# A decoder layer on one core: where the last query head's means, the sample constants and the low key halves are placed, and how sums of sample pairs are split up

## The chip, the cores and the metric

The kernel runs on one core of a Trainium2 chip. Its time is the device time of one execution in microseconds, as the median of the runs. All arithmetic is in the kernel; the host only lays arrays out.

## The reference

One layer of a hybrid decoder with shared weights for two groups of requests: a prompt of 1024 tokens (batch 1) and 8 sampling requests of 8 tokens each with 4096 cached positions. Everything is float32, the model width is 1024. Cut to what matters:

```python
h = rms_norm(x, norm1) * (1 + scale1) + shift1          # scale, shift: from a conditioning vector
z = h @ w_in
q, kc, vc, ks, vs, kw, vw, gates, conv_bg, conv_cg, conv_h, pool_in = split(z)
q  = rms_norm(q per head of 64, q_gain); ks, kw likewise
k_cmp, v_cmp = compress(all raw keys / values, blocks of 32, stride 16)
o_cmp, p_cmp = cmp_attention(q, k_cmp, v_cmp)
top_i, ok    = select_blocks(p_cmp)                      # 16 blocks of 64 keys
o_slc = slc_attention(q, top_i, ok, ks, vs)
o_win = window_attention(q, kw, vw)                      # 512 positions
o = g0 * o_cmp + g1 * o_slc + g2 * o_win
x = x + gate1 * (concat[o, short_conv, multi_pool] @ w_out)
x = x + gate2 * swiglu(rms_norm(x, norm2) * (1 + scale2) + shift2)
```

There are 8 query heads and 2 key heads. A prompt token sees at most 16 blocks, so selection keeps them all there; a sample token selects 16 of 65.

## The kernel before

The kernel is written against a framework that tracks tiles, places semaphores, allocates buffers and finally orders each engine's instructions by a simulated timeline, in which an instruction traced earlier goes first among those ready. Two things bend that order: a block under `high_priority` counts as traced 2000 instructions earlier, and `issue_after(ins)` puts what a block traces on the engine of `ins` behind `ins` on that engine.

The order of tracing comes from a small planner in the kernel. Every part is a generator. It yields the time at which it can go on, by a model of the engines' times (`use` adds a cost to an engine); `run` resumes the part of lowest priority number that is ready by TensorE's model time, and moves that time on where none is. `hold(test)` yields until a test is true, in steps of 0.25 us.

Matrix products in full precision use three products of halves: `split` makes a high half by a copy to the type fp32r on ScalarE (L175) and a low half by a subtraction (`combine`, L171), on VectorE unless told otherwise.

The stages are:

1. The front: norm and modulation of h, in three chunks of tokens (384, 384 and 320 columns).
2. The input projection. For each of 16 weight tiles of 128 output channels and each chunk, `project` accumulates 8 x 3 products in one bank. The last four tiles are q0 to q3, each of two query heads. Each chunk of a query or key tile then goes through `head_norm`: squares (ScalarE, L757), means by a product with a constant matrix `mean_h` (TensorE), root (ScalarE, L762), reciprocal (VectorE, L765), and scaling (VectorE, L766), which reads the projection's bank again. `heads` counts these, `last_scale` is the last scaling. Meanwhile compression (`compress`) of cached pages goes on, three of eight batches in this stage.
3. Attention. `attention` makes the masks (GpSimd and VectorE), `key_stacks` splits the two sets of prompt keys (j = 0 selection, j = 1 window; 1024 columns and 64 compressed ones each) into `kh` and `kl`, `query_parts` splits the queries of a tile of 128 tokens into `qh` and `ql`. `constants3` makes masks and index matrices for the sample tokens (`rsum`, `m_new`, `m_win`, `sel`, `hind`), `sample_setup` lays out their queries and new keys (`qb`, `kn`). Then three parts share the engines:
   - the prompt: 32 units (8 query tiles, 2 halves of the heads, selection or window branch). `scores` runs the products into banks of the tag S (six of them), evacuates them with mask and minimum (VectorE, L1123), then exponential (ScalarE, L1135), reciprocal and gate (VectorE), and scales the probabilities (GpSimd, L1145). `values` transposes them and multiplies by the values.
   - the compression of the other five batches, whose products read `stream`.
   - the samples, in four pairs of requests: `sample_select` scores the compressed keys and selects blocks; 9 units per pair score pages of `cacheB` (tiles `unit` and `stream`); `sample_combine` weights the pair's eleven partial sums into `co` (L1437) and stores them. The units of a pair begin when `combined` shows that the pair before is done.
4. The output projection and the feed-forward part.

Tiles named `P` (probabilities) are allocated in a pool that opens where the projected keys lay. The planner's choice among the three parts of attention follows changing priorities, for example `1.8 + v_done / 32` for the prompt and `2 + 1.1 * u_done / 36` for the samples.

Of the kernel before, what the change touches and what calls it, by code (L numbers as in the profile page):

```python
# [17 lines left out]
P = 128  # L18
# [26 lines left out]
PACE = 0.5  # L45
EPS = 1e-6
# [16 lines left out]
class Kernel:  # L63
# [218 lines left out]
    def constants3(self, c):  # L282
        nc = self.nc
        with self.pool("ctmp") as tp:

            ti = tp.tile([P, 1], I32, name="ti")
            nc.gpsimd.iota(ti, pattern=[[0, 1]], base=0, channel_multiplier=1)
            t7 = tp.tile([P, 1], I32, name="t7")
            nc.vector.tensor_scalar(t7, ti, 7, None, op0=OP.bitwise_and)
            tv = tp.tile([P, 1], F32, name="tv")  # L290
            nc.vector.tensor_copy(tv, t7)


            di = tp.tile([P, P], I32, name="di")
            nc.gpsimd.iota(di, pattern=[[1, P]], base=P, channel_multiplier=-1)
            d7 = tp.tile([P, P], I32, name="d7")
            nc.vector.tensor_scalar(d7, di, 7, None, op0=OP.bitwise_and)
            eq = tp.tile([P, P], F32, name="eq")
            nc.vector.tensor_scalar(eq, d7, 0.0, None, op0=OP.is_equal)
            self.rsum = c.tile([P, P], F32, name="rsum")  # L300
            nc.gpsimd.memset(self.rsum, 0.0)
            for q in range(4):
                s = slice(32 * q, 32 * q + 32)
                nc.vector.tensor_copy(self.rsum[s, s], eq[s, s])


            a = tp.tile([P, 4, 64], F32, name="a")
            for b2 in range(2):
                nc.gpsimd.iota(a[64 * b2:64 * b2 + 64], pattern=[[-16, 4], [1, 64]], base=-8 * b2,
                               channel_multiplier=0, allow_small_or_imprecise_dtypes=True)  # L310
            ge = tp.tile([P, 4, 64], F32, name="ge")
            nc.vector.tensor_scalar(ge, a, 0.0, None, op0=OP.is_ge)
            ok = tp.tile([P, 4, 64], F32, name="ok")
            nc.vector.scalar_tensor_tensor(ok, a, tv[:, 0:1], ge, op0=OP.is_le, op1=OP.mult)
            self.m_new = c.tile([P, 4, 64], F32, name="m_new")
            nc.vector.tensor_scalar(self.m_new, ok, -1.0, 1e30, op0=OP.add, op1=OP.mult)


            w = tp.tile([P, 8], F32, name="w")
            nc.gpsimd.iota(w, pattern=[[1, 8]], base=0, channel_multiplier=0, allow_small_or_imprecise_dtypes=True)  # L320
            self.m_win = c.tile([P, 512], BF16, name="m_win")
            nc.gpsimd.memset(self.m_win, 0.0)
            nc.vector.tensor_scalar(self.m_win[:, 0:8], w, tv[:, 0:1], NEG, op0=OP.is_le, op1=OP.mult)


            self.sel = c.tile([P, 4, P], F32, name="sel")
            si = tp.tile([P, 4, 2, 8, 8], F32, name="si")
            for p in range(4):
                nc.gpsimd.iota(si[:, p], pattern=[[-8, 2], [0, 8], [-1, 8]], base=-64 - 16 * p,
                               channel_multiplier=1, allow_small_or_imprecise_dtypes=True)  # L330
            nc.vector.tensor_scalar(self.sel.rearrange("a p r -> a (p r)"), si.rearrange("a p b g t -> a (p b g t)"),
                                    0.0, None, op0=OP.is_equal)


            hi = tp.tile([P, 8], F32, name="hi")
            for b2 in range(2):
                nc.gpsimd.iota(hi[64 * b2:64 * b2 + 64], pattern=[[-8, 8]], base=0, channel_multiplier=1,
# [2037 lines left out]
```

## Time and profile before

| | |
|---|---|
| median of 3 runs | 1656.8 us (1656.56 to 1657.72) |
| the profiled execution | 1654.03 us, span 1652.4 us |
| granted TensorE clock, mean over the span | 0.981 |
| busy: PE, PEld | 1565.2, 1388.2 us |
| busy: DVE, ACT, POOL | 1092.2, 775.7, 656.3 us |
| end of the input projection | 366.9 us |
| first prompt scores | 378.5 us |
| last sample products of attention | 815.8 us |

A profile shows one execution. Engines are PE (TensorE's products), PEld (its weight loads), DVE (VectorE), ACT (ScalarE), POOL (GpSimd) and SP, which issues transfers. A row of the timeline gives start, duration, engine, line, operation, the tile written and the tiles read, shapes and a count, and in brackets how long the engine had been idle before it and what ended that. L139 is the line of all plain products, L143 that of transposes, L171 and L175 those of all subtractions and copies of `split`.

### The profile page before, as it was taken

How to read it: one execution, taken by the hardware profiler on the slowest of the kernel's cores; microseconds unless marked ns; L12 is line 12 of the kernel's file. 1: busy time of each engine (PE TensorE's matmuls, PEld its weight loads, DVE VectorE, ACT ScalarE, POOL GpSimd, SP SyncE). 2: the span in 40 equal slices, each digit the busy share in tenths (PEclk: the TensorE clock that was granted, in tenths of full speed). 3: DMA queues.
4: the chain of work that ended last, by engine and by line, in shares of the span. 5: the costliest groups of instructions: out<-in, count | busy, mean ns of one | idle time of the engine just before them, and what ended most of it. 6: DMA issues, size and time to landing. Idle time of an engine off the chain costs nothing.

```text
span 1652.4 us, 35479 instructions
## 1 busy us (share of the span) xinstructions
PE 1565.2 (95%) x12569; PEld 1388.2 (84%) x12569; DVE 1092.2 (66%) x2645; ACT 775.7 (47%) x1828; POOL 656.3 (40%) x789
## 2 busy tenths in 40 slices
PE   6999999997999899899999989999999999899998
PEld 2899997895777666566699989999999999899998
DVE  4713224876555666767589878777777775577668
ACT  3522215434765667656576534343434333344444
POOL 3111110213333133222213356554544554788765
PEclk9999999998999899999999999999999999999999
DMA  9576665425467373244696565336443335967643
GB/s 339 188 266 188 193 182 169 147 77 163 136 179 219 108 211 97 78 132 126 194 319 213 189 224 185 139 137 232 147 146 138 138 136 199 380 244 249 217 159 125
DMA packets 194659, 302.12 MB, mean 183 GB/s; under 512 B 25841, under 2 KB 131634, under 8 KB 194162
## 3 DMA queue, kind: packets, MB, share of 16 engines
q1 hardware_dynamic: 175346, 272.17, 49.5%
q0 software_dynamic: 6208, 17.38, 3.3%
q10 hardware_dynamic: 12928, 10.29, 2.1%
q8 instruction: 100, 1.64, 0.4%
q14 instruction: 77, 0.63, 0.1%
HBM read 233.43 MB, written 70.53 MB: 184 GB/s over the span
## 4 chain that ended last, share of the span: by engine, by line
PE 74%; DVE 11%; ACT 5%; DMA 4%; issue 3%; POOL 2%; SPq 0%; ACTq 0%; DVEq 0%; POOLq 0%
PE bank L139 70%; PE bank L143 4%; DVE P L1123 2%; ACT P L1135 2%; DVE w_lo L171 1%; DMA w_raw<-in_wup 1%; DMA w_raw<-in_wout 1%; ACT w_hi L175 1%; DMA x<-x_d 1%; POOL P L1145 1%; POOL b_t L171 1%; DMA x<-in_xT 1%; DVE h_lo L474 1%; DVE b_lo L171 0%; DVE ml L171 0%
## 5 line engine op out<-in xcount | busy, mean ns | idle before, releaser
L139 PE MATMUL bank<-b_hi,w_hi 128*128 128x272 f32 x1232 | 351.3, 290 | 7.0 <-DVE pair L1722 2.9
L139 PE MATMUL bank<-b_lo,w_hi 128*128 128x272 f32 x1232 | 353.5, 289 | 1.7 <-DVE b_lo L171 1.7
L139 PE MATMUL bank<-b_hi,w_lo 128*128 128x272 f32 x1232 | 348.8, 288 | 1.3 <-DVE w_lo L171 0.9
L139 PEld LDWEIGHTS bank<-b_hi,w_hi 128*128 128x128 f32 x1232 | 230.5, 189 | 10.4 <-ACT b_hi L175 4.0
L139 PEld LDWEIGHTS bank<-b_lo,w_hi 128*128 128x128 f32 x1232 | 232.4, 189 | 2.4 <-DVE b_lo L171 2.3
L139 PEld LDWEIGHTS bank<-b_hi,w_lo 128*128 128x128 f32 x1232 | 230.6, 189 | 1.8 <-DVE w_lo L171 1.1
L1145 POOL TENSOR_SCALAR P<-P,st 128x128 f32<-128x128 f32 (+10 forms) x192 | 109.1, 582 | 232.7 <-DVE st L1141 141.3
L171 DVE TENSOR_TENSOR w_lo<-w_raw,w_hi 128x512 fp32r<-128x512 f32 (+2 forms) x120 | 114.6, 965 | 81.8 <-ACT w_hi L175 81.6
L171 POOL TENSOR_TENSOR w_s<-w_raw 128x512 f32<-128x512 f32 (+1 forms) x88 | 124.3, 1412 | 70.3 <-DVE w_lo L171 53.4
L175 ACT ACTIVATE w_hi<-w_raw 128x512 fp32r<-128x512 f32 (+2 forms) x122 | 80.6, 677 | 132.5 <-PE bank L139 87.7
L139 PEld LDWEIGHTS bank<-stream 128*128 128x128 f32 x1056 | 128.8, 200 | 16.0 <-issue 11.9
L139 PE MATMUL bank<-stream 128*128 128x128 f32 x1056 | 135.1, 286 | 1.8 <-DMA stream<-in_cacheA 1.1
L1135 ACT ACTIVATE P<-P,st 128x128 f32<-128x128 f32 (+12 forms) x192 | 112.7, 588 | 45.8 <-DVE st L1129 28.6
L171 POOL TENSOR_TENSOR x<-x,d_m 128x272 f32<-128x272 f32 x136 | 118.0, 887 | 34.2 <-DVE x L1925 17.5
L139 PE MATMUL bank<-h_hi,w_hi 128*128 128x384 f32 (+1 forms) x384 | 129.4, 337 | 0.4 <-DVE q L766 0.4
L139 PE MATMUL bank<-h_hi,w_lo 128*128 128x384 f32 (+1 forms) x384 | 126.6, 330 | 0.0
L139 PE MATMUL bank<-h_lo,w_hi 128*128 128x384 f32 (+1 forms) x384 | 126.4, 329 | 0.0
L171 DVE TENSOR_TENSOR w_lo<-w_s,w_hi 128x512 fp32r<-128x512 f32 (+1 forms) x124 | 115.7, 935 | 15.9 <-ACT w_hi L175 13.7
L139 PE MATMUL bank<-g,w_hi 128*128 128x272 f32 x616 | 121.4, 293 | 4.7 <-DVE x L1925 4.7
L139 PE MATMUL bank<-g,d_hi 128*128 128x272 f32 x616 | 119.1, 289 | 2.3 <-DVE x L1928 1.6
L1925 DVE SCALAR_TENSOR_TENSOR x<-bank,mod,x 128x272 f32<-128x272 f32 (+1 forms) x200 | 90.2, 476 | 39.1 <-PE bank L139 28.2
L175 ACT ACTIVATE w_hi<-w_s 128x512 fp32r<-128x512 f32 (+1 forms) x124 | 76.6, 621 | 64.5 <-PE bank L139 35.4
(376 smaller groups left out, 3756.3 us busy)
## 6 DMA issues: line engine op xcount, KB each, us to landing
g<-g_d SPq DMA_DIRECT2D x63, 544.0 KB, 6.1
g_d<-f_s SPq DMA_DIRECT2D x57, 544.0 KB, 3.4
wada<-in_wada SPq DMA_DIRECT2D x96, 256.0 KB, 5.3
stream<-in_cacheA SPq DMA_DIRECT2D x192, 128.0 KB, 3.2
w_raw<-in_wup SPq DMA_DIRECT2D x40, 512.0 KB, 4.3
unit<-in_cacheB SPq DMA_DIRECT2D x152, 128.0 KB, 2.4
stream<-in_cacheB SPq DMA_DIRECT2D x104, 128.0 KB, 2.2
w_raw<-in_wout SPq DMA_DIRECT2D x24, 512.0 KB, 5.7
```

Source lines behind the costliest of these rows:

```text
L139: return self.nc.tensor.matmul(out, lhsT, rhs, start=start, stop=stop, skip_group_check=chain)
L143: return self.nc.tensor.transpose(out, in_, self.ident if ident is None else ident)
L171: (self.nc.vector if eng == "dve" else self.nc.gpsimd).tensor_tensor(out, a, b, op=op)
L175: self.last_hi = self.nc.scalar.activation(hi, src, AF.Copy)
L474: nc.vector.scalar_tensor_tensor(lk, t, sh[:, k, 0:1], hk.bitcast(F32), op0=OP.add, op1=OP.subtract)
L1123: nc.vector.tensor_tensor_reduce(out=Pt[:, 2 * g + hl, col:col + n], in0=S[g][:, p0:p0 + n], in1=mk, scale=-1.0, scalar=3e38, op0=OP.add, ...
L1135: nc.scalar.activation(Ps, Ps, AF.Exp, scale=-1.0, bias=sy[:, g, 0:1], accum_out=sy[:, g, 1:2])
L1145: nc.gpsimd.tensor_scalar(Ps, Ps, sy[:, g, 3:4], 0.0, op0=OP.mult, op1=OP.add)
L1925: self.last_gate = nc.vector.scalar_tensor_tensor(out[:, :n], acc[:, :n], self.mod[:, 5, m, 0:1], out[:, :n], op0=OP.mult, op1=OP.add)
```

## The change

Six edits:

- `PINNED = ("q3",)`: for the last query tile, `project` is called for half of the accumulation steps; then the part holds until one more head norm has been traced, and the second half is put behind that norm's mean product (`last_mean`) on TensorE.
- `query_parts` for query tile 0 is traced ahead of `key_stacks`.
- In `key_stacks`, the low halves of the window keys (j = 1) are made on GpSimd.
- `constants3` is traced behind the second score group of the first unit, its VectorE instructions behind that group's last evacuation (`first_evac`); its scratch tiles lie in the pool of attention instead of one of their own. The sample part starts when they are traced.
- A pair's selection waits until the pair before has been selected (`selected`).
- For the first three pairs, `sample_combine` yields ahead of every third of the eleven sums.

```diff
+PINNED = ("q3",)
...
     def constants3(self, c):
         nc = self.nc
-        with self.pool("ctmp") as tp:
+        tp = c
...
-    def project(self, w, h, ch, n):
-        acc = self.bank()
-        for k in range(KT):
+    def project(self, w, h, ch, n, acc=None, ks=range(KT)):
+        acc = self.bank() if acc is None else acc
+        for k in ks:
...
-            self.mm(m[:, :n], self.mean_h, sq[:, :n], True, True)
+            self.last_mean = self.mm(m[:, :n], self.mean_h, sq[:, :n], True, True)
...
-                        acc = self.project(w, h, ch, n)
+                        if nm in PINNED:
+                            heads = self.heads
+                            acc = self.project(w, h, ch, n, None, range(KT // 2))
+                            yield from self.hold(lambda: self.heads > heads)
+                            with self.tc.issue_after(self.last_mean.ins):
+                                self.project(w, h, ch, n, acc, range(KT // 2, KT))
+                        else:
+                            acc = self.project(w, h, ch, n)
...
-                self.split(kh[:, a:a + n], kl[:, a:a + n], src, n)
+                self.stacks_at = self.split(kh[:, a:a + n], kl[:, a:a + n], src, n, eng="pool" if j else "dve")
                 yield max(self.t["dve"], self.t["act"]) - 1.0
-        self.stacks_at = max(self.t["dve"], self.t["act"])
...
+            if u == 0 and hl == 1:
+                self.first_evac = self.last_evac
+                self.scored = True
...
-        yield from self.hold(lambda: self.cmp_done >= 2 * p + 2)
+        yield from self.hold(lambda: self.cmp_done >= 2 * p + 2 and self.selected == p)
...
-        for c in range(11) if p < 3 else (8, 10, 0, 1, 2, 3, 4, 5, 6, 7, 9):
+        self.use("dve", 1.3, self.t["pe"])
+        for x, c in enumerate(range(11) if p < 3 else (8, 10, 0, 1, 2, 3, 4, 5, 6, 7, 9)):
+            if p < 3:
+                if x % 3 == 0:
+                    yield self.t["dve"]
+                self.use("dve", 0.35, self.t["pe"])
             nc.vector.scalar_tensor_tensor(o, part[:, c], w[:, c:c + 1], o, op0=OP.mult, op1=OP.add)
-        r = self.use("dve", 4.0, self.t["pe"]) + 0.5
         if p < 3:
-            yield r
+            yield self.t["dve"] + 0.3
...
     def attention(self, ap, kp_, opened):
         self.masks(ap)
         self.use("dve", 1.0)
+        self.query_parts(ap, 0)
         yield from self.key_stacks()
-        self.query_parts(ap, 0)
         with self.tc.issue_after(self.last_scale.ins):
-            self.constants3(ap)
             self.sample_setup(ap)
-        self.use("dve", 5.0)
         kp_.__exit__(None, None, None)
         pp = opened.enter_context(self.pool("prompt"))
         self.spawn(lambda: 1.8 + self.v_done / 32, self.prompt_attention(pp))
+        yield from self.hold(lambda: self.scored)
+        with self.tc.issue_after(self.first_evac.ins):
+            self.constants3(ap)
+        self.use("dve", 3.2)
+        self.constants_done = True
...
         sp = opened.enter_context(self.pool("samp", "left"))
+        yield from self.hold(lambda: self.constants_done)
         yield self.t["dve"]
```

More of the change, by code (lines that the diff above doesn't have):

```diff
@@ L283, in constants3 @@
         nc = self.nc
-        with self.pool("ctmp") as tp:
[L286 to L337, printed above, removed]
-                               allow_small_or_imprecise_dtypes=True)
-            hg = tp.tile([P, 8], F32, name="hg")
-            nc.vector.tensor_scalar(hg, hi, 0.0, None, op0=OP.is_ge)
-            self.hind = c.tile([P, 8], F32, name="hind")
-            nc.vector.scalar_tensor_tensor(self.hind, hi, 7.0, hg, op0=OP.is_le, op1=OP.mult)
@@ new lines, in constants3 @@
+        tp = c
+        ti = tp.tile([P, 1], I32, name="ti")
+        nc.gpsimd.iota(ti, pattern=[[0, 1]], base=0, channel_multiplier=1)
+        t7 = tp.tile([P, 1], I32, name="t7")
+        nc.vector.tensor_scalar(t7, ti, 7, None, op0=OP.bitwise_and)
+        tv = tp.tile([P, 1], F32, name="tv")
+        nc.vector.tensor_copy(tv, t7)
+        di = tp.tile([P, P], I32, name="di")
+        nc.gpsimd.iota(di, pattern=[[1, P]], base=P, channel_multiplier=-1)
+        d7 = tp.tile([P, P], I32, name="d7")
@@ new lines, in constants3 @@
+        nc.vector.tensor_scalar(d7, di, 7, None, op0=OP.bitwise_and)
+        eq = tp.tile([P, P], F32, name="eq")
+        nc.vector.tensor_scalar(eq, d7, 0.0, None, op0=OP.is_equal)
+        self.rsum = c.tile([P, P], F32, name="rsum")
+        nc.gpsimd.memset(self.rsum, 0.0)
+        for q in range(4):
+            s = slice(32 * q, 32 * q + 32)
+            nc.vector.tensor_copy(self.rsum[s, s], eq[s, s])
+        a = tp.tile([P, 4, 64], F32, name="a")
+        for b2 in range(2):
+            nc.gpsimd.iota(a[64 * b2:64 * b2 + 64], pattern=[[-16, 4], [1, 64]], base=-8 * b2,
+                           channel_multiplier=0, allow_small_or_imprecise_dtypes=True)
@@ new lines, in constants3 @@
+        ge = tp.tile([P, 4, 64], F32, name="ge")
+        nc.vector.tensor_scalar(ge, a, 0.0, None, op0=OP.is_ge)
+        ok = tp.tile([P, 4, 64], F32, name="ok")
+        nc.vector.scalar_tensor_tensor(ok, a, tv[:, 0:1], ge, op0=OP.is_le, op1=OP.mult)
+        self.m_new = c.tile([P, 4, 64], F32, name="m_new")
+        nc.vector.tensor_scalar(self.m_new, ok, -1.0, 1e30, op0=OP.add, op1=OP.mult)
+        w = tp.tile([P, 8], F32, name="w")
+        nc.gpsimd.iota(w, pattern=[[1, 8]], base=0, channel_multiplier=0, allow_small_or_imprecise_dtypes=True)
@@ new lines, in constants3 @@
+        self.m_win = c.tile([P, 512], BF16, name="m_win")
+        nc.gpsimd.memset(self.m_win, 0.0)
+        nc.vector.tensor_scalar(self.m_win[:, 0:8], w, tv[:, 0:1], NEG, op0=OP.is_le, op1=OP.mult)
+        self.sel = c.tile([P, 4, P], F32, name="sel")
+        si = tp.tile([P, 4, 2, 8, 8], F32, name="si")
+        for p in range(4):
+            nc.gpsimd.iota(si[:, p], pattern=[[-8, 2], [0, 8], [-1, 8]], base=-64 - 16 * p,
+                           channel_multiplier=1, allow_small_or_imprecise_dtypes=True)
@@ new lines, in constants3 @@
+        nc.vector.tensor_scalar(self.sel.rearrange("a p r -> a (p r)"), si.rearrange("a p b g t -> a (p b g t)"),
+                                0.0, None, op0=OP.is_equal)
+        hi = tp.tile([P, 8], F32, name="hi")
+        for b2 in range(2):
+            nc.gpsimd.iota(hi[64 * b2:64 * b2 + 64], pattern=[[-8, 8]], base=0, channel_multiplier=1,
+                           allow_small_or_imprecise_dtypes=True)
+        hg = tp.tile([P, 8], F32, name="hg")
+        nc.vector.tensor_scalar(hg, hi, 0.0, None, op0=OP.is_ge)
@@ L346, in ada_setup @@
+        self.hind = c.tile([P, 8], F32, name="hind")
+        nc.vector.scalar_tensor_tensor(self.hind, hi, 7.0, hg, op0=OP.is_le, op1=OP.mult)
     def ada_setup(self, pool):
@@ L2186, in build @@
         self.combined = 0
+        self.scored = self.constants_done = False
         self.n2_done = 0
@@ L2221, in build @@
         self.post_free = True
+        self.selected = 0
         self.constants2()
```

3 lines of the change are left out of this document (2 added, 1 removed).

## The prediction

> **What bounds the kernel now.** I read the page first, then the busy times of each engine by stretches of 50 us, then finer stretches where TensorE fell behind, then the waits and the timeline of that place, engine by engine.
>
> ```profile
> PE 1565.2 (95%) x12569; PEld 1388.2 (84%) x12569; DVE 1092.2 (66%) x2645; ACT 775.7 (47%) x1828; POOL 656.3 (40%) x789
> ```
>
> TensorE is busy 1565.2 us, 95% of a span of 1652.4, so time can come only from its idle 87 us and from stretches in which its clock is low. Every part of the change but the spread sums acts at the passage from the input projection to attention, so I cut that passage where its engine changes: waiting, first scores, and the work behind them. Columns are busy time (and instructions) of PE, PEld, DVE, ACT and POOL, then the granted clock, the DMA share and GB/s.
>
> ```profile
> 372.00:378.50 6.50, 0.00 (x0) 0.03 (x1) 6.50 (x9) 0.00 (x0) 3.65 (x14) 0.86 0.68 203
> 378.50:383.20 4.70, 1.98 (x15) 1.67 (x15) 4.54 (x31) 0.19 (x1) 0.00 (x0) 0.50 0.77 227
> 383.20:393.10 9.90, 9.90 (x77) 9.66 (x77) 4.02 (x34) 5.41 (x25) 5.01 (x14) 0.81 0.48 145
> ```
>
> For 6.5 us TensorE does nothing while VectorE never stops; in the next 4.7 us it works 1.98 us at half clock. That is the only stage of the kernel where VectorE sets the pace outright. The waits between 350 and 395 us name what ended TensorE's two pauses (total, times, longest), and the timeline shows where they lie:
>
> ```profile
> PE bank L139 <- DVE q L766: 6.6, 1, 6.6
> ...
> PE bank L139 <- DVE st L1123: 2.7, 1, 2.7
> ```
>
> ```profile
> 366.86 1.50 PE L139 MATMUL bank<-h_sq,mean_h 128*128 128x384 f32 x4
> 368.19 3.73 PE L139 MATMUL bank<-stream 128*128 128x128 f32 x32
> 378.50 0.89 PE L139 MATMUL bank<-kh,qh 64*128 64x192 f32 x2 [6.58 <-DVE q L766]
> ...
> 383.18 0.44 PE L139 MATMUL bank<-kh,qh 64*128 64x128 f32 x1 [2.71 <-DVE st L1123]
> ...
> 384.61 8.53 PE L139 MATMUL bank<-stream 128*128 128x128 f32 x64
> ```
>
> So 9.3 us are idle: first the scores wait for the normalised query of L766 (through the accumulator bank it reads: the operands for query tile 0 were ready before), then for the first softmax evacuation of L1123, which frees a bank. The four mean matmul pieces at 366.86 are those of q3's second and third chunk, both behind the whole projection. ScalarE and VectorE show why L766 is late:
>
> ```profile
> 363.83 0.48 ACT L757 ACTIVATE h_sq<-bank 128x384 f32<-128x384 f32 x1
> 367.06 0.44 ACT L757 ACTIVATE h_sq<-bank 128x320 f32<-128x320 f32 x1 [2.74 <-PE bank L139]
> 367.39 1.05 ACT L175 ACTIVATE kh<-kv__98 128x1024 fp32r<-128x1024 f32 x1
> ...
> 370.62 0.98 ACT L762 ACTIVATE h_sq<-bank,eps 128x384 f32<-128x384 f32 x2
> ```
>
> ```profile
> 368.47 1.23 DVE L171 TENSOR_TENSOR kl<-kv__98,kh 128x1024 fp32r<-128x1024 f32 x1 [1.30 <-ACT kh L175]
> ...
> 370.86 1.16 DVE L171 TENSOR_TENSOR kl<-kv__98,kh 128x1024 fp32r<-128x1024 f32 x1
> ...
> 373.37 4.55 DVE L765 RECIPROCAL h_sq<-h_sq 128x384 f32<-128x384 f32 x2
> 377.85 0.97 DVE L766 SCALAR_TENSOR_TENSOR q<-bank,qgain_s,h_sq 128x384 f32<-128x384 f32 x2
> 378.74 0.14 DVE L289 TENSOR_SCALAR t<-ti 128x1 int32<-128x1 int32 x1
> ...
> 379.67 0.48 DVE L1223 MEMSET qb<- 128x512 f32 x1
> 380.08 0.15 DVE L1230 COPY kn<-kv__98 128x128 f32<-128x128 f32 x1
> ...
> 380.55 0.57 DVE L1226 COPY qb<-q 64x256 f32<-64x256 f32 x2
> ...
> 382.65 0.28 DVE L1123 CUSTOM_DVE_ANT_0 P<-bank,m_slc 128x128 f32<-128x128 f32 x1
> ```
>
> The second chunk is squared by 364.31, yet its mean runs at 366.86 and its root at 370.62, behind all key splits on ScalarE's queue. VectorE then works without a pause from 368.47 to the first evacuation at 382.65: low key parts, two reciprocals, two scalings, the sample constants.
>
> **The change part by part.** All terms are against the profiled execution, 1654.0 us with a span of 1652.4 and 1.6 around it; the median of the runs, 1656.8, is 2.8 us more, and I put the difference on that median.
>
> *Pinned means.* The third chunk of q3 takes the 3.2 us between the squares' starts at 363.83 and 367.06. With the second chunk's mean in its middle, that mean runs near 365.0, after its square's end at 364.31, so TensorE doesn't stop; the matmuls are the same in number and cost nothing more. The root (half of 0.98, 0.5) then ends by 366.3, ahead of the splits, and one reciprocal with its scaling, (4.55 + 0.97) / 2 = 2.8, goes into the time in which VectorE waited before 368.47. By 369.2 they are done; the first low key part would have started at 368.47, so 0.7 of the 2.8 comes back. Worth 2.1 on VectorE's chain. The third chunk's mean can't be pinned to anything and stays late: its root still stands behind the splits, and it is what is late next. If the second half waited for a square delayed on ScalarE, TensorE would stop by that delay, at most the 1.05 of one split; none stands there, so I take 0 (bounds: 1.05 lost, nothing won beyond the 2.8).
>
> *Queries of tile 0 ahead of the key stacks.* The same two instructions, earlier on ScalarE and VectorE, move the key split by about half of 1.05. It is inside the 0.7; 0.
>
> *Low halves of the window keys on GpSimd.* VectorE loses the 1.16 at 370.86 and the small 64-column piece. Nearest row for the price on GpSimd, the same subtraction 1120 wide, by form:
>
> ```profile
> L171 POOL TENSOR_TENSOR wt_lo<-stream,wt_hi 128x1120 fp32r<-128x1120 f32 x2 | 5.1, 2572 | 18.5 <-ACT wt_hi L175 18.5
> ```
>
> That is 2.35 us for 1024 columns. Its first reader is the window unit behind the two first score groups, and the prompt's probability tiles lie where those keys lay, so VectorE's first evacuation now waits for GpSimd as well. GpSimd's masks fill it from the end of the projection to about 372, so the low keys are there by 374.5, before the evacuation that I expect below: gain 1.2. The price against it is that the two engines get in each other's way:
>
> ```profile
> 370.81 1.24 POOL L279 TENSOR_SCALAR_AFFINE_SELECT rowok<-rowok 128x1 f32<-128x1 f32 x1
> ```
>
> One element per lane takes 1.24 us, from 370.81 to 372.05, exactly while VectorE's subtraction of two tiles ran (370.86 to 372.02). Turned round, a 2.35 us subtraction on GpSimd can hold VectorE's own two-input work. VectorE has such work for only part of that stretch (the reciprocal has one input), so I take 1.0, with 0 and 2.35 as ends. [...]
>
> *Sample constants behind the first softmax pass.* From 378.74 to 382.65 are 3.9 us; the copies of sample queries and keys that stay take 0.48 + 0.15 + 0.57 = 1.2. So 2.7 us leave the path to the first evacuation. They come back behind it, ahead of some reciprocals of the first softmax; the 8.53 us of compression matmuls at 384.61 cover that. Were that cover gone, they would cost their 2.7. Their GpSimd instructions are ordered behind nothing and only fill that engine. The sample stream waits for the constants, so its page loads on SP's queue are issued a few us later. The timeline of that queue, and the instructions on the tile they fill (least, median and longest ns, first and last start):
>
> ```profile
> 375.51 9.82 SPq L530 DMA_DIRECT2D unit<-in_cacheB  x16
> ```
>
> ```profile
> L139 PE MATMUL bank<-unit,qb x84: 589/593/1112, 408.2 to 809.8; 128*64 128x512 f32 x84
> ```
>
> Issued from 375.51, first read at 408.2: a delay below some 20 us costs 0.
>
> *Sums in threes, and selections one after another.* The same instructions, in four groups with other work between. By form:
>
> ```profile
> L1437 DVE SCALAR_TENSOR_TENSOR co<-part,cw,co 128x128 f32<-128x128 f32 x44 | 18.8, 426 | 1.1
> ```
>
> One pair's eleven are 4.7 us of VectorE at a time when the prompt's evacuations also want it. Around the second pair's sums TensorE waited once, 2.56 us:
>
> ```profile
> 685.58 1.21 PE L143 MATMUL bank<-ident,P 64*128 64x64 f32 x32 [2.56 <-POOL P L1145]
> ```
>
> Three pairs are spread, so up to 7.7 us could be won if each had such a stall and lost it, and as much lost if the spread sums made one each. Most of the sums already had evacuations between them, so I take 0. The selections' order follows from buffers anyway: 0.
>
> *Sum.* VectorE's chain to the first evacuation shortens by 2.1 + 1.2 - 1.0 + 2.7 = 5.0 us, to about 377.7. TensorE's idle 9.3 us is bounded by that chain, so 5.0 of it goes and 4.3 stays. The clock: 1.98 us of work in the second stretch ran at 0.50 and 9.9 in the third at 0.81, so 1.0 + 1.9 = 2.9 us were lost to it. With pauses of 2 to 3 us instead of 6.6 and 2.7, I take half, 1.4 (0 and 2.9 as ends). [...] Total 6.4: 1654.0 - 6.4 = 1647.6 for a profiled execution, 1650.4 on the median. From 385 us on, all orders are laid out anew by the planner; I let the shift pass through, since TensorE remains the engine with the most work.
>
> **The rivals.** *Hardly any gain.* The third chunk's late mean, root and reciprocal set the first scores as before, and GpSimd blocks VectorE for the whole 2.35; constants are paid behind the evacuation (2.7). Left: 2.1 + 1.2 - 2.35 + 2.7 - 2.7 = 1.0, no clock gain: 1655.8. For it: the first wait is for L766, one of which still comes last. Against: one reciprocal instead of two stands there.
>
> *More gain.* Both pauses close down to what the compression matmuls can fill: 9.3 + 2.9 = 12.2 us, 1644.6. For it: 3.73 and 8.53 us of such matmuls stand ready. Against: they are bound to page loads.
>
> *Slower.* The sums in threes, spread over more softmax passes, meet GpSimd's scaling of probabilities and hold it, and TensorE waits for that, as at 685.58. Each costs 2.56; with three pairs in four groups there are twelve places. To end 3.3 us above the old time it takes 6.4 + 3.3 = 9.7 us, four such stalls; five would give 1656.8 - 6.4 + 12.8 = 1663.2. For it: their mean of 426 ns holds some much longer ones. Against: the sums met the scaling before, too.
>
> **How the numbers follow.** Likeliest, 0.57: 1650.4, own range 1647 to 1653.5 (the port price and the clock from end to end). More gain 0.11, hardly any 0.19, slower 0.13. What a measurement here can tell from no change is about 0.2%, 3.3 us: faster 0.68, same 0.19, slower 0.13. The range goes from 1644, the largest gain, to 1661, short of most of the slower case.
>
> **What would show it.** Right: two mean pieces of q3's second chunk stand between its third chunk's projection matmuls; only one reciprocal of L765 behind the key splits; L171 with tile kl on POOL at about 2.4 us; L1123 first near 377 instead of 382.65, with the lines of the constants behind it; TensorE's two pauses together near 4 us. Wrong: a pause that names POOL kl, a first evacuation after 380, or gains at 380 us that are gone again when attention ends near 815.

## The result, and the profile after

The changed kernel takes 1671.1 us (median of six runs, 1666.8 to 1673.0) against 1657.2 for the kernel before beside it: a ratio of 1.0081, 95% interval 1.0057 to 1.0104. It is slower by 0.8%, where 0.4% faster was forecast and the range ended at 1661. The profiled execution takes 1672.9 us. Every line number is shifted (products L139 to L140, transposes L143 to L144, subtractions L171 to L172, evacuation L1123 to L1131, scaling of the query L766 to L768).

The passage came out as forecast. TensorE's timeline there, then VectorE's, then GpSimd's:

```profile
364.10 0.81 PE L140 MATMUL bank<-h_sq,mean_h 128*128 128x384 f32 x2
364.45 0.60 PE L140 MATMUL bank<-h_hi,w_hi 128*128 128x320 f32 x1
...
367.19 0.81 PE L140 MATMUL bank<-h_sq,mean_h 128*128 128x320 f32 x2 [0.53 <-ACT h_sq L759]
367.83 3.73 PE L140 MATMUL bank<-stream 128*128 128x128 f32 x32
371.50 0.36 PE L140 MATMUL bank<-kh,qh 64*128 64x192 f32 x2
...
374.45 0.32 PE L140 MATMUL bank<-kh,qh 64*128 64x128 f32 x1 [2.04 <-DVE q L768]
376.35 0.44 PE L140 MATMUL bank<-kh,qh 64*128 64x128 f32 x1 [1.58 <-DVE st L1131]
```

```profile
369.10 1.22 DVE L172 TENSOR_TENSOR kl<-kv__98,kh 128x1024 fp32r<-128x1024 f32 x1
...
371.67 2.14 DVE L767 RECIPROCAL h_sq<-h_sq 128x320 f32<-128x320 f32 x1
373.85 0.55 DVE L768 SCALAR_TENSOR_TENSOR q<-bank,qgain_s,h_sq 128x320 f32<-128x320 f32 x1
...
374.85 0.30 DVE L1241 COPY kn<-kv__98 128x128 f32<-128x128 f32 x1
...
375.82 0.29 DVE L1131 CUSTOM_DVE_ANT_0 P<-bank,m_slc 128x128 f32<-128x128 f32 x1
```

```profile
372.72 2.34 POOL L172 TENSOR_TENSOR kl<-kv__98,kh 128x1024 fp32r<-128x1024 f32 x1
```

The second chunk's mean (two pieces) stands inside the third chunk's products, one reciprocal is left behind the key split, the first evacuation comes at 375.82 instead of 382.65, and the idle 9.3 us have become 0.53 + 2.04 + 1.58 = 4.15.

The loss lies behind that. SyncE's queue, and TensorE's products on the samples' tile (least, median and longest ns, first and last start):

```profile
371.60 20.19 SPq L532 DMA_DIRECT2D stream<-in_cacheA  x18
392.41 9.30 SPq L532 DMA_DIRECT2D unit<-in_cacheB  x16
```

```profile
L140 PE MATMUL bank<-unit,qb x76: 592/592/1112, 428.8 to 814.3; 128*64 128x512 f32 x76
```

The first pages of the samples are issued at 392.41, behind 18 loads for the compression, instead of at 375.51 behind six; the first sample unit is scored at 428.8 instead of 408.2. For the stages I use the same cut for all kernels: the passage (355 to 400), two stretches of attention, and the rest up to the first product of the output projection. Columns are length, then busy time of PE, PEld, DVE, ACT and POOL, granted clock, DMA share, GB/s. First before, then after:

```profile
355.00:400.00 45.00, 35.71 (x250) 31.77 (x249) 32.56 (x120) 18.27 (x67) 16.90 (x47) 0.86 0.43 130
400.00:560.00 160.00, 152.07 (x1424) 118.35 (x1424) 86.22 (x364) 99.89 (x272) 49.24 (x101) 0.98 0.55 168
560.00:720.00 160.00, 143.88 (x1476) 92.19 (x1473) 115.75 (x517) 107.53 (x294) 52.42 (x81) 0.96 0.40 118
720.00:816.90 96.90, 88.53 (x967) 58.80 (x964) 59.03 (x216) 56.21 (x141) 20.86 (x28) 0.96 0.48 147
```

```profile
355.00:400.00 45.00, 38.37 (x288) 33.98 (x287) 32.28 (x127) 22.12 (x79) 19.49 (x53) 0.92 0.39 118
400.00:560.00 160.00, 144.78 (x1321) 112.27 (x1323) 83.41 (x354) 99.58 (x266) 47.45 (x97) 0.97 0.58 175
560.00:720.00 160.00, 142.23 (x1465) 91.50 (x1463) 106.43 (x468) 100.60 (x267) 46.76 (x72) 0.91 0.39 117
720.00:833.76 113.76, 98.86 (x1032) 64.97 (x1029) 73.15 (x278) 67.30 (x173) 29.38 (x40) 0.93 0.43 131
```

I call "lost" what TensorE is idle plus its busy time multiplied by one minus the clock. It is a rough count (the mean clock of a stretch is laid on all its work), good for comparing kernels and not for adding up to the microsecond. In the passage it falls from 14.3 to 9.7 us; in the three later stretches it rises from 11.0, 21.9 and 11.9 to 19.6, 30.6 and 21.8. (The cut at 400 splits TensorE's 4.48 us wait that ends at 402.00 in the changed kernel; the note below the table of experiments says what follows from that.) The output projection starts at 833.76 instead of 816.90. TensorE's longest waits from 400 to 840 (total, times, longest):

```profile
PE bank L144 <- POOL P L1153: 12.3, 7, 3.2
PE bank L140 <- ACT pair L624: 7.3, 4, 4.5
PE bank L140 <- DMA unit<-in_swinKV: 6.7, 1, 6.7
PE bank L140 <- ACT w_hi L176: 5.6, 1, 5.6
PE bank L140 <- DVE pair L589: 2.9, 1, 2.9
PE bank L140 <- ACT spt L162: 2.7, 1, 2.7
```

The first was there before (12.1 us, six times). The others are new or longer: compression that waits for its own post-processing (`pair`), at 402 and 449, while no sample work exists to fill in; the load of the window pages `swinKV`, at 567; the last sample unit, alone at the end (`spt`), and the output weights (`w_hi`), whose raw tiles lie where the `stream` tiles lay and so can be loaded only when the last sample units have left those.

### The profile page after: what moved, and what is told of

Same layout as the page of the kernel before. It is cut to its first block, busy times and chain, and to the rows that moved or that the text cites. A ratio compares the mean times of both kernels' runs of the same rounds, so it can differ in the third digit from the quotient of the medians.

```text
span 1671.3 us, 35457 instructions
## 1 busy us (share of the span) xinstructions
PE 1568.5 (94%) x12569; PEld 1389.9 (83%) x12569; DVE 1089.3 (65%) x2643; ACT 779.1 (47%) x1827; POOL 658.5 (39%) x791
## 5 line engine op out<-in xcount | busy, mean ns | idle before, releaser
L140 PE MATMUL bank<-b_hi,w_hi 128*128 128x272 f32 x1232 | 351.6, 291 | 7.9 <-DVE pair L1742 2.9
L140 PE MATMUL bank<-b_lo,w_hi 128*128 128x272 f32 x1232 | 353.7, 289 | 2.5 <-DVE b_lo L172 2.5
L140 PE MATMUL bank<-b_hi,w_lo 128*128 128x272 f32 x1232 | 348.9, 288 | 1.4 <-DVE w_lo L172 1.4
L140 PEld LDWEIGHTS bank<-b_hi,w_hi 128*128 128x128 f32 x1232 | 231.0, 189 | 10.9 <-ACT b_hi L176 4.8
L140 PEld LDWEIGHTS bank<-b_lo,w_hi 128*128 128x128 f32 x1232 | 232.9, 189 | 3.4 <-DVE b_lo L172 3.4
L140 PEld LDWEIGHTS bank<-b_hi,w_lo 128*128 128x128 f32 x1232 | 230.9, 189 | 1.7 <-DVE w_lo L172 1.7
L1153 POOL TENSOR_SCALAR P<-P,st 128x640 f32<-128x640 f32 (+11 forms) x192 | 109.0, 581 | 236.4 <-DVE st L1149 130.3
L172 DVE TENSOR_TENSOR w_lo<-w_raw,w_hi 128x512 fp32r<-128x512 f32 (+2 forms) x120 | 114.1, 960 | 85.7 <-ACT w_hi L176 85.3
L172 POOL TENSOR_TENSOR w_s<-w_raw 128x512 f32<-128x512 f32 (+1 forms) x88 | 125.1, 1422 | 71.8 <-DVE w_lo L172 51.8
L140 PEld LDWEIGHTS bank<-stream 128*128 128x128 f32 x1056 | 126.8, 198 | 17.1 <-issue 13.1
L140 PE MATMUL bank<-stream 128*128 128x128 f32 x1056 | 133.6, 284 | 4.5 <-DVE pair L589 2.9
L1143 ACT ACTIVATE P<-P,st 128x640 f32<-128x640 f32 (+10 forms) x192 | 113.0, 590 | 45.1 <-DVE st L1131 24.2
L140 PE MATMUL bank<-h_hi,w_hi 128*128 128x384 f32 (+1 forms) x384 | 130.2, 339 | 0.4 <-DVE q L768 0.4
L172 POOL TENSOR_TENSOR x<-x,d_m 128x272 f32<-128x272 f32 x136 | 116.8, 880 | 32.6 <-DVE x L1945 18.8
L172 DVE TENSOR_TENSOR w_lo<-w_s,w_hi 128x512 fp32r<-128x512 f32 (+1 forms) x124 | 117.0, 945 | 16.3 <-ACT w_hi L176 14.1
L140 PE MATMUL bank<-g,w_hi 128*128 128x272 f32 x616 | 121.4, 292 | 6.3 <-DVE x L1945 6.3
L140 PE MATMUL bank<-h_hi,w_lo 128*128 128x384 f32 (+1 forms) x384 | 126.2, 329 | 0.0
L140 PE MATMUL bank<-h_lo,w_hi 128*128 128x384 f32 (+1 forms) x384 | 126.2, 329 | 0.0
L140 PE MATMUL bank<-g,d_hi 128*128 128x272 f32 x616 | 119.0, 289 | 1.3 <-DVE x L1948 1.3
L140 PEld LDWEIGHTS bank<-g,w_hi 128*128 128x128 f32 x616 | 98.9, 192 | 6.8 <-DVE x L1945 6.7
```

The source lines that it names most:

```text
L140: return self.nc.tensor.matmul(out, lhsT, rhs, start=start, stop=stop, skip_group_check=chain)
L172: (self.nc.vector if eng == "dve" else self.nc.gpsimd).tensor_tensor(out, a, b, op=op)
L1143: nc.scalar.activation(Ps, Ps, AF.Exp, scale=-1.0, bias=sy[:, g, 0:1], accum_out=sy[:, g, 1:2])
L1153: nc.gpsimd.tensor_scalar(Ps, Ps, sy[:, g, 3:4], 0.0, op0=OP.mult, op1=OP.add)
```

## The experiments

Ratios are to the kernel before, run beside each. "Early" and "late" say when the sample part starts; "lost" is given for the four stages of the table above, in the kernel's own profile. Where the text says how much of the "order" is kept, it means the share of the rows of TensorE's instruction order in attention that stand in the same sequence in the other kernel.

| kernel | start | us | ratio (95%) | lost, by stage |
|---|---|---|---|---|
| before | early | 1657.2 | 1 | 14.3, 11.0, 21.9, 11.9 |
| changed | late | 1671.1 | 1.0081 (1.0057 to 1.0104) | 9.7, 19.6, 30.6, 21.8 |
| e1 pages early, constants late | early (see e1) | 1672.5 | 1.0112 (1.0088 to 1.0136) | 7.7, 16.4, 37.8, 14.5 |
| e2 constants in the old place | early | 1660.1 | 1.0024 (1.0008 to 1.0040) | 11.4, 17.3, 23.6, 13.1 |
| e3 before, late samples | late | 1679.4 | 1.0128 (1.0102 to 1.0154) | 16.2, 34.4, 25.1, 9.8 |
| e4 sums whole | late | 1673.9 | 1.0109 (1.0087 to 1.0131) | 7.6, 23.0, 20.4, 25.2 |
| p1 before, plan | early | 1656.4 | 1.0000 (0.9988 to 1.0012) | 14.7, 11.5, 27.7, 11.2 |
| b108 before, plan | early | 1651.6 | 0.9980 (0.9966 to 0.9994) | 14.7, 13.5, 17.3, 9.7 |
| bk1 before, plan | early | 1654.9 | 0.9992 (0.9978 to 1.0006) | 14.6, 15.6, 16.0, 10.1 |
| bm4 before, plan | early | 1660.5 | 1.0026 (1.0015 to 1.0037) | 14.7, 10.2, 31.5, 13.9 |
| a108 changed, plan | late | 1683.2 | 1.0154 (1.0131 to 1.0176) | 7.4, 24.0, 29.8, 30.2 |
| am3 changed, plan | late | 1661.4 | 1.0033 (1.0022 to 1.0044) | 13.1, 24.7, 16.4, 19.3 |
| q4 passage alone | early | 1668.0 | 1.0070 (1.0052 to 1.0088) | 12.3, 12.4, 24.4, 18.1 |
| q4_108 passage, plan | early | 1655.3 | 0.9993 (0.9979 to 1.0007) | 12.2, 12.7, 23.8, 10.5 |
| q4_m3 passage, plan | early | 1654.3 | 1.0000 (0.9983 to 1.0016) | 12.2, 19.8, 18.6, 9.0 |
| u1 unpinned | late | 1670.0 | 1.0084 (1.0069 to 1.0099) | 8.4, 22.0, 31.5, 19.8 |
| f1 last units elsewhere | late | 1672.2 | 1.0093 (1.0063 to 1.0124) | 9.2, 21.5, 30.9, 28.6 |
| f2 `swinKV` on GpSimd's queue | late | 1671.2 | 1.0090 (1.0063 to 1.0118) | 11.8, 20.2, 28.4, 19.3 |
| f3 both | late | 1675.9 | 1.0119 (1.0093 to 1.0146) | 8.2, 25.3, 25.9, 27.1 |
| f4 am3 and f1 | late | 1660.6 | 1.0039 (1.0020 to 1.0059) | 9.5, 25.0, 16.5, 27.3 |

The first of the four numbers has to be read with care. The passage lies up to 5 us earlier or later from one kernel's profile to another's (first evacuation at 373.20 in am3, at 378.55 in a108), so the fixed cut at 400 catches different waits at its end: in am3 a whole one of 4.62 us for `pair`, in the changed kernel a part of one. Counted from the square of q3's third chunk (ScalarE, 367.06 before, 366.70 in the changed kernel), the passage hardly varies: the first evacuation comes 15.59 or 15.60 us behind it in the six kernels without edits there (before, p1, b108, bk1, bm4, e3), and 9.12 to 9.14 us in the nine with the pin, the low keys on GpSimd and the late constants (changed, e1, e4, a108, am3, f1 to f4).

**Early pages (e1).** The wait for the constants moves from the start of the sample part to the first selection, behind its loads:

```diff
-        yield from self.hold(lambda: self.constants_done)     # in sample()
...
+        yield from self.hold(lambda: self.constants_done)     # in sample_select, behind the loads of kvc
```

> The changed kernel, but the sample part starts as before: its first page loads are issued without waiting for the constants, and only the first selection of blocks waits for them. Theory A (late start: the changed kernel's sample loads stand behind 12 more compression loads on SP's queue, the first sample unit is scored at 428.8 instead of 408.2 us, the samples end alone and the output projection starts 16.9 us later): the first sample unit is scored near 408 us again, the output projection starts at 811 to 818 us, and the time is 1648 to 1658. Theory B (the sums in threes hold the scaling of probabilities): no change to speak of, 1667 to 1673. Theory C (no one edit: any new order of the work of attention costs or brings some us): anything from 1650 to 1680.

The loads went where they had been, and the first unit is scored at 398.2, but the time stayed, and the output projection starts at 834.61, not at 811 to 818 (the first row is SyncE's queue, the other two are the stages):

```profile
374.64 9.56 SPq L532 DMA_DIRECT2D unit<-in_cacheB  x16
```

```profile
355.00:400.00 45.00, 40.56 (x298) 35.42 (x297) 32.66 (x148) 22.14 (x81) 20.25 (x54) 0.92 0.46 138
...
560.00:720.00 160.00, 137.33 (x1339) 88.14 (x1341) 98.94 (x448) 103.07 (x262) 47.13 (x71) 0.89 0.37 110
```

So Theory A as I had it, page loads behind page loads, falls. The passage lost 7.7 us here, and 37.8 us went in a stretch 200 us later. The first selection isn't late either. The products that score the compressed keys for the selections (least, median and longest ns, first and last start), in the kernel before, the changed one and e1:

```profile
L139 PE MATMUL bank<-kvc,qb x16: 378/430/634, 397.0 to 700.6; 128*64 128x256 f32 x16
L140 PE MATMUL bank<-kvc,qb x16: 379/404/431, 410.4 to 694.1; 128*64 128x256 f32 x16
L140 PE MATMUL bank<-kvc,qb x16: 379/382/430, 388.1 to 699.5; 128*64 128x256 f32 x16
```

In e1 loads, first selection (388.1) and first unit (398.2) are all earlier than in the kernel before (397.0 and 408.2), and still it loses 1.1%. TensorE's longest waits there, from 560 to 720, are for GpSimd's scaling of the probabilities, 14.1 us against 7.2 before:

```profile
PE bank L144 <- POOL P L1153: 14.1, 4, 5.6
```

**Constants in the old place (e2).**

```diff
         with self.tc.issue_after(self.last_scale.ins):
+            self.constants3(ap)
             self.sample_setup(ap)
+        self.use("dve", 5.0)
+        self.constants_done = True
...
-        yield from self.hold(lambda: self.scored)
-        with self.tc.issue_after(self.first_evac.ins):
-            self.constants3(ap)
-        self.use("dve", 3.2)
-        self.constants_done = True
```

> The changed kernel with the sample constants traced where they were, ahead of the first scores; the other edits stay. Theory A: the sample part starts early, so 1650 to 1660, and worse than the early loads alone by up to 2.7 us (the constants are on VectorE's chain to the first evacuation again, which moves from 375.8 to about 378.5). Theory B: 1667 to 1673. Theory C: anything from 1650 to 1680.

This one edit brings the ratio from 1.0081 down to 1.0024, some 9 us (1660.1). The constants are back on VectorE's way to the first evacuation, which comes 12.23 us behind the square instead of 9.12. The later stages:

```profile
400.00:560.00 160.00, 145.58 (x1373) 112.75 (x1373) 80.45 (x357) 103.36 (x281) 50.12 (x102) 0.98 0.54 165
560.00:720.00 160.00, 145.10 (x1458) 92.17 (x1454) 110.81 (x489) 104.37 (x276) 47.20 (x73) 0.94 0.40 116
720.00:821.93 101.93, 91.58 (x991) 60.05 (x986) 63.81 (x228) 60.24 (x153) 25.74 (x34) 0.97 0.50 152
```

Against the changed kernel, 2.3, 7.0 and 8.7 us less are lost in these stretches.

**The late start alone (e3),** in the kernel before:

```diff
         sp = opened.enter_context(self.pool("samp", "left"))
+        yield from self.hold(lambda: self.scored)
```

> The kernel before, with one thing of the change alone: the sample part starts only when the second score group of the first unit has been traced. All else is as before. Theory A: slower by most of what the change lost plus what its passage gained, 1664 to 1676, with the output projection near 830 to 840 us instead of 816.9. Theory B: as before, 1654 to 1660. Theory C: anything from 1650 to 1680.

Even a little slower than expected, 1679.4, and the loss begins at once:

```profile
400.00:560.00 160.00, 139.57 (x1225) 108.79 (x1224) 75.31 (x344) 91.72 (x265) 47.04 (x98) 0.90 0.54 163
```

34.4 us are lost here instead of 11.0; the first unit is scored at 447.6.

**The sums in one piece (e4)** (the eleven sums and their one booking of 4.0 us as before):

> The changed kernel with each pair's eleven sums in one piece, as before; the late start of the samples stays. Theory A: 1666 to 1673, the output projection near 830 to 836 us. Theory B: most of the loss goes, 1650 to 1658. Theory C: anything from 1650 to 1680.

No gain: in this kernel the spread sums did no harm, and e2 has them too, at 1.0024. Theory B falls here, and with it the cause that the prediction's rival "slower" gave.

**Is it any new order? (p1, b108, a108, q4).** Theory C now says that the order before was a good one among many. Each of the first three kernels changes one number of the planner and no instruction; q4 is the kernel before with the pin, the queries first and the low keys on GpSimd.

```diff
-        self.use("dve", 5.0)
+        self.use("dve", 6.0)                                             # p1
...
-        self.spawn(lambda: 2 + 1.1 * self.u_done / 36, self.sample_attention(sp))
+        self.spawn(lambda: 2 + 1.08 * self.u_done / 36, self.sample_attention(sp))   # b108, a108, q4_108
```

> The kernel before, with one number of the planner's model changed (the cost booked on VectorE behind the sample constants, 6.0 for 5.0 us). No instruction is added or removed; the passage and the start of the samples stay; only the order of the work of attention differs. Theory C (the kernel before had an order of attention that happens to have few stalls, and almost any other order loses some of that): 1660 to 1675. Theory D (late constants and a late start of the sample part cost their own price, whatever the order): as before, 1653 to 1659.

> The kernel before, with the samples' priority changed by a hair (2 + 1.08 x for 2 + 1.1 x, x from 0 to 1): the same instructions, another order from some way into attention on. Theory C: 1660 to 1675. Theory D: 1653 to 1659.

> The changed kernel with the same small change of the samples' priority (2 + 1.08 x). Passage and late start as in the changed kernel. Theory C: anything from 1650 to 1675, as likely below the changed kernel as above it. Theory D: 1667 to 1673.

> The kernel before with the edits of the passage alone: the last query head's means pinned, the first queries ahead of the key stacks, the low window keys on GpSimd. The sample constants stay where they were, sums and selections too. The first evacuation should come near 379, 3.5 us earlier than before. Theory D: that gain passes through, 1651 to 1655. Theory C: the order of attention is new, so 1657 to 1672.

The kernel before did not lose: p1 is equal (97% of its order is the old one, so it tells little), b108 (75%) is 0.2% faster. The changed kernel lost another 12 us by the same number. And q4 did lose, 0.7%, though its samples start early; its first evacuation came 2.0 us earlier behind the square than before (13.59 for 15.59), not 3.5. Theory C misses p1 and b108, Theory D misses q4, and a108 lies above the range of both.

**Orders further away (bk1, bm4, am3), and the pin (u1).** In bk1, bm4 and am3 about half of the order or less is kept; in u1 nearly all of it.

```diff
-        share = lambda: 1.9 + 0.4 * (self.cmp_done - EARLY) / (NB - EARLY)
+        share = lambda: 1.9 + 0.36 * (self.cmp_done - EARLY) / (NB - EARLY)   # bk1
...
-        self.spawn(lambda: 1.8 + self.v_done / 32, self.prompt_attention(pp))
+        self.spawn(lambda: 1.78 + self.v_done / 32, self.prompt_attention(pp)) # bm4; 1.82 in am3, f4, q4_m3
...
-PINNED = ("q3",)
+PINNED = ()                                                                 # u1
```

> The kernel before, with the growth of the compression's priority at 0.36 instead of 0.4. The same instructions, the same passage and the same start of the samples; from some 120 groups of matmuls into attention the order is another, and only half of it still runs in the old sequence (in the two nudged kernels before it was 97% and 75%). Theory C (an order of attention that is laid out anew costs some 10 us against the old one, whatever laid it out): 1660 to 1680. Theory D (it is the edits themselves): 1652 to 1659.

> The kernel before, with the prompt's priority starting at 1.78 instead of 1.8. Same instructions, passage and start; a little under half of attention's order is the old one. Theory C: 1660 to 1680. Theory D: 1652 to 1659.

> The changed kernel with the prompt's priority starting at 1.82 instead of 1.8; all edits stay, less than half of attention's order is that of the changed kernel. Theory C: anything from 1655 to 1683, with no tie to the changed kernel's 1671. Theory D: 1667 to 1675.

> The changed kernel without the pinned means. Its order of attention is the changed kernel's but for a few rows, so this measures the pin alone: by the prediction's own step it is worth 2.1 us on VectorE's chain, so the first evacuation goes from 375.8 to about 378 and the time to 1671 to 1675. By Theory C that passes through, because the order is kept; if the pin itself cost something further on, this would be faster than the changed kernel.

The strong form of Theory C falls: a new order of the kernel before costs between nothing and 0.3%. Theory D misses too: one order of the changed kernel (am3) gets within 0.3% of the kernel before, and bm4, at 1660.5, lies just above its range. The pin makes the first evacuation 2.2 us earlier (11.32 us behind the square without it, 9.12 with), but TensorE's idle time in the passage only 0.7 us shorter (4.15 with it, and in u1 one pause):

```profile
376.69 0.39 PE L140 MATMUL bank<-kh,qh 64*128 64x192 f32 x1 [4.87 <-DVE q L768]
```

The time does not tell the two kernels apart; 2.2 us is 0.13%, less than either interval leaves open.

**The named waits (f1 to f4).** f1 puts the last two sample units into `unit` tiles, f2 issues the first pair's `swinKV` load on GpSimd's queue, f3 does both, f4 is f1 on am3; f1 to f3 keep 97 to 99% of the order.

```diff
             src = self.unit_free.pop(0)
+            if src == "stream" and self.unit_next >= 34:
+                continue
...
-            self.nc.sync.dma_start(kv.rearrange("p (b t) f -> p b t f", b=2),
+            (self.nc.sync if p else self.nc.gpsimd).dma_start(kv.rearrange("p (b t) f -> p b t f", b=2),
```

> The changed kernel, with the last two sample units loaded into tiles named unit instead of stream, so that the first output weights, which lie where the stream tiles lay, can be loaded earlier; the order of attention up to there is kept. Theory W (the loss lies in named waits): the 5.64 us wait for w_hi goes and the clock there (0.66 from 820 to 840) comes back in part: 1661 to 1667. Theory C in its strong form (the loss is spread over the order, the waits at the end only use time that something else would take): 1669 to 1673.

> The changed kernel, with the load of the first pair's swinKV issued on GpSimd's queue instead of SP's, where it stands behind 18 page loads. Order otherwise kept. Theory W: the 6.66 us wait at 567 goes, with some of the clock (0.74 from 560 to 600): 1661 to 1667. Theory C, strong form: 1669 to 1673.

> Both edits in the changed kernel. Theory W: the two gains add up, 1652 to 1661. Theory C, strong form: 1669 to 1673.

> The changed kernel with the prompt's priority starting at 1.82 (1661 in its own run) and the last two sample units in unit tiles. Theory W: its wait for w_hi (5.6 us) goes: 1652 to 1657, about the kernel before. Theory C, strong form: 1660 to 1663.

None gained, and f3, at 1675.9, lies above the ranges of both theories. The waits were not taken away but moved. In f1 the wait for `w_hi` is gone, and the last units, with two tiles to load into instead of five, wait instead: their pages are issued at 819.47 instead of 803.44, behind three loads of output weights (SyncE's queue in the changed kernel, one row, and in f1, two; then TensorE's timeline in f1):

```profile
803.44 5.51 SPq L532 DMA_DIRECT2D stream<-in_cacheB  x8
...
804.05 14.73 SPq L1543 DMA_DIRECT2D w_raw<-in_wout  x3
819.47 4.32 SPq L532 DMA_DIRECT2D unit<-in_cacheB  x8
```

```profile
824.27 4.06 PE L140 MATMUL bank<-unit,qb 128*64 128x512 f32 x4 [4.29 <-DMA unit<-in_cacheB]
...
841.33 1.97 PE L140 MATMUL bank<-unit,spt 128*64 128x128 f32 x16 [5.23 <-ACT spt L162]
```

What f1 loses by starting the output projection later (843.23 for 833.76) it gets back behind it (829.3 us to the end instead of 837.5), so the last of the four numbers says little for f1, f3 and f4.

In f2 the window pages come no earlier; they are read at 566.93 instead of 567.34, though f2's passage lies 2.3 us earlier as a whole, and TensorE's 6.66 us of waiting have split into 1.49 and 3.96:

```profile
561.89 1.08 PE L140 MATMUL bank<-pt,vt__291 128*64 128x256 f32 x8 [1.49 <-DVE st L1131]
566.93 1.97 PE L140 MATMUL bank<-unit,qb 128*64 128x512 f32 x4 [3.96 <-DMA unit<-in_swinKV]
```

These runs therefore do not measure what the waits are worth.

**The passage without the late start, in two more orders (q4_108, q4_m3).**

> The passage-only kernel with the samples' priority 2 + 1.08 x, the number with which the kernel before ran at 1651.6. Constants and samples start early. Theory L (the late constants and samples cost the changed kernel its time; the passage edits gain a few us, and 1668 is an unlucky order): 1647 to 1658. Theory P (the passage edits themselves disturb attention): 1662 to 1672.

> The passage-only kernel with the prompt's priority starting at 1.82; only some four tenths of attention's order are those of the passage-only kernel before. Theory L: 1647 to 1660. Theory P: 1662 to 1672.

Both equal the kernel before, so 1668 was that order, and Theory P falls. The gain of some us that Theory L adds does not show: with the constants still ahead of the first evacuation the passage loses 12.2 us in both instead of 14.3, and 2 us is below what the runs tell.

**Together.** Nine kernels start the samples early: the kernel before, p1, b108, bk1 and bm4 (mean ratio 1.0000), and q4, q4_108, q4_m3 and e2, which carry the edits of the passage (mean 1.0022). Five that differ in order start them late: the changed kernel, e3, e4, a108 and am3 (mean 1.0101). In the late ones 19.6 to 34.4 us are lost from 400 to 560, in the early ones 10.2 to 19.8. With e1, which is early by its times, the ten early ones have a mean of 1.0020. The groups overlap: e1 (1.0112) and q4 (1.0070) are early and lie above am3 (1.0033), which is late. So a late start costs some 0.8% in the mean over these orders, and an order alone can cost as much. Nor does the loss from 400 to 560 decide the time: am3 loses 24.7 us there, q4 12.4.

## Why the prediction was wrong

- Pinned means, low keys on GpSimd, constants behind the first softmax: right in place, and a little too small in size. The first evacuation was forecast "about 377.7" and came at 375.82; counted from the square of the third chunk, 6.5 us were won on VectorE's chain (15.59 to 9.12) where 5.0 were forecast. The constants are 3.1 of these (e2), forecast 2.7, and the pin 2.2 (u1), forecast 2.1; the 1.2 that is left is the low keys' forecast gain with next to no price. TensorE's idle time did not follow the chain one to one: it fell by 5.1, to 4.15, and the pin gave it 0.7 of its 2.2. That "4.3 stays" came out is luck, a larger gain on the chain and a smaller share of it for TensorE.
- The price of GpSimd beside VectorE, 1.0 (0 to 2.35), the "port price" of the forecast's range: next to nothing of it shows, and no run shows a port. GpSimd's subtraction took 2.34 us, as forecast from the 1120-wide one (2.35), and VectorE's scaling of 320 columns inside it 0.55, as long as the 0.97 for two chunks of 384 and 320 allow. Inside those 2.34 us VectorE has no subtraction of two tiles: the reciprocal reads one, and the scaling has one of its two in an accumulator bank. In the kernel before such a subtraction did take longer beside GpSimd, later on (VectorE's timeline, then GpSimd's):

```profile
1223.57 0.69 DVE L171 TENSOR_TENSOR w_lo<-w_s,w_hi 128x512 fp32r<-128x512 f32 x1 [0.30 <-ACT w_hi L175]
...
1224.90 0.44 DVE L1722 TENSOR_TENSOR f_v<-bank,f_v 128x272 f32<-128x272 f32 x1
...
1230.51 0.43 DVE L1722 TENSOR_TENSOR f_v<-bank,f_m 128x272 f32<-128x272 f32 x1
...
1233.55 1.78 DVE L171 TENSOR_TENSOR w_lo<-w_s,w_hi 128x512 fp32r<-128x512 f32 x1
```

```profile
1225.48 0.77 POOL L1752 TENSOR_TENSOR pair<-pair,f_v 128x272 f32<-128x272 f32 x1 [8.93 <-DVE f_v L1722]
...
1230.01 1.21 POOL L171 TENSOR_TENSOR f_T<-pair,f_T 128x272 f32<-128x272 f32 x1
...
1233.01 1.77 POOL L171 TENSOR_TENSOR w_s<-w_raw 128x512 f32<-128x512 f32 x1
```

The subtraction of two tiles took 0.69 us with GpSimd idle and 1.78 beside GpSimd's of 1.77, the operation with an input in a bank 0.44 with GpSimd idle and 0.43 beside it. In the changed kernel the copy of the samples' new keys (`kn`), begun at 374.85, 0.21 us before GpSimd's subtraction ended, took 0.30 us; it took 0.15 before, at 380.08 with GpSimd idle, and 0.16 in u1 at 377.46.
- The clock, 1.4 us back, by the author's estimate half of 2.9: hardly any came. The three stretches behind the first pause, in which 0.37, 3.60 and 3.00 us of work ran at 0.57, 0.50 and 0.74, lose 0.2 + 1.8 + 0.8 = 2.8 us to it, where the prediction counted 2.9 before (the last section cuts the stretches more closely and shows that this depends on the execution):

```profile
374.45:376.40 1.95, 0.37 (x3) 0.26 (x3) 1.90 (x15) 0.24 (x1) 1.95 (x4) 0.57 0.62 184
376.40:380.00 3.60, 3.60 (x21) 3.48 (x22) 3.57 (x37) 3.60 (x22) 0.11 (x2) 0.50 0.24 73
380.00:383.00 3.00, 3.00 (x22) 3.00 (x21) 1.80 (x13) 0.48 (x4) 2.15 (x7) 0.74 0.00 0
```

- The sums in threes at 0: right in the changed kernel (e4 without them is no faster).
- The step that failed is in the part on the sample constants: "The sample stream waits for the constants, so its page loads on SP's queue are issued a few us later", and "a delay below some 20 us costs 0". The loads were not a few us but 16.9 us later, because the planner laid 12 more compression loads ahead of them. And the sum priced only the loads. What waits for the constants is the start of a whole part of attention, scores, selections and all. While it is missing, TensorE has the prompt and the compression alone, both with waits of their own, and at the end of the changed kernel the samples are left alone (not of e3, whose last stage loses 9.8 us). In place of 0, e3, which is the kernel before with this one delay, measures 1.28%, some 21 us; putting the constants and with them the start back in the changed kernel (e2) brings 1.0081 down to 1.0024.
- With it fell "I let the shift pass through, since TensorE remains the engine with the most work", which put the new order of attention at nothing. That TensorE is the bound on average did not mean that idle time saved in one place stays saved: am3, the changed kernel, e4, e1 and a108 have the same passage within 0.02 us from square to first evacuation and ran at 1.0033, 1.0081, 1.0109, 1.0112 and 1.0154. "Gains at 380 us that are gone again when attention ends near 815" stood among the signs of being wrong, and that is what happened.

What stays open: how much of the changed kernel's own 0.8% is the late start and how much its order. e1 starts loads, first selection and first units as early as the kernel before and still loses 1.1%; only one order of it ran, and it did not run with the sums in one piece, so that its 14.1 us of waiting for the scaling, the wait that the prediction's slower case named, may or may not come from them. By which of the new waits the late start costs its time isn't settled either, since the edits that were to remove them moved them. And the early and late kernels differ in more than the start: their ratios go from 0.9980 to 1.0112 and from 1.0033 to 1.0154.

The fastest kernel of the study is b108, the kernel before with one priority at 1.08: 0.9980 (0.9966 to 0.9994), ahead of both. No kernel with the edits of the passage was measurably faster than the kernel before.

## What to carry to other kernels

When an edit moves the start of one of several parts that share an engine, price the part, not its first load: ask what fills the engine until it comes, and what is left alone at the end. Where a planner lays out an order anew, time several orders of each variant by changing a number that means nothing; here one and the same set of edits ran at 1.0070, 0.9993 and 1.0000, and a single run of each would have condemned or acquitted it by chance. Taking away a wait in the profile is not shown until the next trace has neither that wait nor its successor.

## What the runs showed of the hardware

In these profiles the granted clock did not follow TensorE's pauses one by one. Cut where it fell to half and where it came back (worked out from windows of 0.5 us, so an estimate to some hundredths), the stretches are, in the changed kernel, in the kernel before (two) and in p1, whose passage is that of the kernel before:

```profile
374.74:381.57 6.83, 5.25 (x29) 5.13 (x29) 6.65 (x60) 4.32 (x24) 2.49 (x7) 0.50 0.27 79
...
376.74:386.98 10.24, 5.76 (x35) 5.36 (x36) 8.61 (x56) 3.96 (x17) 0.78 (x3) 0.50 0.75 230
397.22:400.64 3.42, 3.42 (x24) 2.76 (x21) 3.19 (x24) 3.09 (x16) 2.57 (x8) 0.50 0.41 123
...
374.88:388.54 13.66, 8.31 (x44) 7.90 (x45) 10.29 (x59) 4.84 (x21) 4.20 (x12) 0.50 0.62 181
```

The passage of before was paid with 10.24 us at half clock in its own profile and with 13.66 in p1's, 2.88 or 4.16 us lost (half of the 5.76 and 8.31 us of work); the changed passage lost 2.63 (half of 5.25). Half is close: in the 3.5 us from 378.00, at 0.50, the changed kernel's trace has 17 products of the compression, in the 3.5 us from 367.90, at 1.00, it has 32. So the clock gave back 0.25 us against the one and 1.53 against the other.

In the changed kernel the clock fell at 374.74, when only the pause of 2.04 us and a product of 0.32 us lay behind it; the pause of 1.58 us came after. In the kernel before it fell at 397.22, behind 9 us (388 to 397) in which TensorE's record, with the ends of products as the profile models them, has no idle time at all:

```profile
388.00:397.00 9.00, 9.00 (x83) 7.44 (x81) 3.49 (x21) 4.08 (x18) 4.53 (x12) 1.00 0.60 183
```

What brought either fall is not shown.
